# A transposing load cut in two: high and low halves of the attention weights in a hybrid decoder step

## The chip, the cores and the metric

The kernel runs on one core of one Trainium2 chip. The metric is the time of one execution on the device in microseconds (us), measured outside the profiler; for the kernel before it is the median of three runs. A profile is one further execution, which has a time and a span (first to last instruction) of its own.

## What is computed

One layer of a decoder trunk, for a prompt of 2048 tokens and for 64 sample tokens (8 sequences of 8). A projection of the normalised input is split among four mixers (differential attention, a gated recurrence, RWKV-7, a diagonal SSM) and a gate; their outputs are concatenated, gated, projected and added to the input. The change touches the prompt's attention alone:

```python
def diff_attn_core(q, k, v, q_pos, k_pos, lam):
    s = jnp.einsum('bqhcd,bkhcd->bhcqk', q, k).astype(jnp.float32) * (A_QK ** -0.5)
    mask = k_pos[None, :] <= q_pos[:, None]
    p = jax.nn.softmax(jnp.where(mask, s, NEG_BIG), axis=-1)
    w = p[:, :, 0] - lam * p[:, :, 1]
    return jnp.einsum('bhqk,bkhd->bqhd', w.astype(v.dtype), v)
```

There are 4 heads, two score maps (c = 0, 1) of width 32 each, and values of width 64. The kernel keeps float32 accuracy out of 16-bit products: a number is split into a 16-bit high part and a 16-bit rest (low part), and high times high, high times low and low times high are added up.

## The kernel before, in words

The program has four stretches. First (to about 280 us of the profile) the input is normalised and q, k and v are projected. Then, to about 1007 us, `attn_prompt` (L317) works through the prompt's attention while `proj_rest` (L583) projects everything else. After that come the sample's attention with the SSM, and last the RWKV mixer with the output projection. The stage that the change touches is the second.

**Attention.** `attn_prompt` loops over 4 heads, and in each over 16 blocks of 128 queries; a call of `attn_rows` (L350) is one such block, called a row here. Row qb sees (qb + 1) * 128 keys, cut into pieces of at most 512 (`PIECE`): rows 0 to 3 have one piece, rows 4 to 7 two, rows 8 to 11 three, rows 12 to 15 four. That is 16 rows of each length over the four heads, 160 pieces and 544 tiles of 128 keys. For each piece TensorE makes two score maps in PSUM (L363), VectorE takes their maxima (L367), ScalarE their exponentials (L371). When all pieces of a row are there, small VectorE instructions work out a factor for each (L374 to L387). Then, piece by piece: GpSimd scales one map (L391), VectorE scales the other and adds (L392), ScalarE casts the sum to float16, the high part, into the left half of tile `a_w` (L395), GpSimd subtracts it and writes the low part into the right half (L396). One transposing DMA, issued on SP's queue, brings both halves back into `a_wt` with the keys on the partitions (L399), since TensorE needs them so. TensorE then multiplies for each tile of 128 keys the high part with the high and low values (L403, 128 columns) and the low part with the high values (L404, 64 columns), all of a row into one PSUM bank `pv`, of which there is a single buffer (`PVB`). ScalarE and VectorE bring the row's result out (L408, L409). `a_w` and `a_wt` have four buffers each.

**What else SP's queue carries in this stage.** The loads of `kh` (L330) at the start of a head and of `qh` (L335) every four rows, the stores of the projections (L608, L634, L643) and of the packed output weights (L1504). SP works through its instructions in order.

**Filler for TensorE.** `proj_rest` makes 10 groups of columns (`FILL`), 2400 matmuls of mostly 512 columns (L206) in this stage. It is paced: each attention matmul of the loops above is noted in a list, `self.anchors`, as many times as it is worth; the filler's position in its own columns gives an index into that list (function `paced`, L1783, with a lag `LEAD`), and every third filler matmul may only be issued after the attention matmul found there. A piece of n tiles puts 2n entries into the list for its scores and 2n for its products.

**The order on each engine** is not written out by hand: the framework's planner (`schedule_with_timeline_sim=True`, L1956) lays out every engine's instructions when the program is built, by its own estimate of when each can start, under the dependencies and the anchors. At run time each engine then keeps to that order.

Of the kernel before, what the change touches and what calls it, by code (L numbers as in the profile page):

```python
# [23 lines left out]
P = 128  # L24
# [29 lines left out]
class Part:  # L54
# [295 lines left out]
    def attn_rows(self, pool, psum, h, qb, q, kh, dst):  # L350
        nc = self.nc
        nk = (qb + 1) * P
        pieces = [(k0, min(PIECE, nk - k0)) for k0 in range(0, nk, PIECE)]
        np_ = len(pieces)
        mx, l, al = (pool.tile([P, T // PIECE, 2], F32, name=f"a_{k}", bufs=3)[:, :np_] for k in ("mx", "l", "al"))
        es = {}
        sig = self.sig[:, h // 2:h // 2 + 1]
        for p, (k0, kn) in enumerate(pieces):
            ss = []
            for c in range(2):  # L360
                s = psum.tile([P, PIECE], F32, name="s", bufs=SB)
                ss.append(s)
                ins = nc.tensor.matmul(s[:, :kn], q[:, c], kh[:, c, k0:k0 + kn], start=True, stop=True)  # L363
                self.anchors += [ins.ins] * (kn // P)
                if k0 + kn == nk:
                    nc.tensor.matmul(s[:, kn - P:kn], self.identb, self.maskn, start=False, stop=True, skip_group_check=True)
                nc.vector.tensor_reduce(mx[:, p, c:c + 1], s[:, :kn], axis=AX.X, op=ALU.max, negate=True)  # L367
            nc.vector.tensor_scalar(mx[:, p], mx[:, p], sig, None, op0=ALU.mult)  # L368
            for c, s in enumerate(ss):
                e = pool.tile([P, PIECE], F32, name="a_e", bufs=AEB)  # L370
                nc.scalar.activation(e[:, :kn], s[:, :kn], AF.Exp, scale=sig, bias=mx[:, p, c:c + 1],  # L371
                                     accum_out=l[:, p, c:c + 1])
                es[p, c] = e
        if np_ == 1:  # L374
            nc.vector.reciprocal(al[:, 0], l[:, 0])
            nc.vector.tensor_tensor(al[:, 0], al[:, 0], self.lamw, op=ALU.mult)
        else:
            mm = pool.tile([P, 2], F32, name="a_mm", bufs=3)
            bc = mm[:, None, :].to_broadcast([P, np_, 2])
            nc.vector.tensor_reduce(mm, mx.rearrange("p n c -> p c n"), axis=AX.X, op=ALU.min)  # L380
            nc.vector.tensor_tensor(mx, mx, bc, op=ALU.subtract)
            nc.scalar.activation(mx, mx, AF.Exp, scale=-1.0)
            nc.vector.tensor_tensor(l, l, mx, op=ALU.mult)
            nc.vector.tensor_reduce(mm, l.rearrange("p n c -> p c n"), axis=AX.X, op=ALU.add)
            nc.vector.reciprocal(mm, mm)
            nc.vector.tensor_tensor(mm, mm, self.lamw, op=ALU.mult)
            nc.vector.tensor_tensor(al, mx, bc, op=ALU.mult)  # L387
        pv = psum.tile([P, 512], F32, name="pv", bufs=PVB)
        for p, (k0, kn) in enumerate(pieces):
            e0, e1 = es[p, 0], es[p, 1]  # L390
            nc.gpsimd.tensor_scalar(e1[:, :kn], e1[:, :kn], al[:, p, 1:2], 0.0, op0=ALU.mult, op1=ALU.add)  # L391
            nc.vector.scalar_tensor_tensor(e0[:, :kn], e0[:, :kn], al[:, p, 0:1], e1[:, :kn],  # L392
                                           op0=ALU.mult, op1=ALU.add)
            w = pool.tile([P, 2 * PIECE], F16, name="a_w", bufs=AWB)[:, :2 * kn]
            nc.scalar.copy(w[:, :kn], e0[:, :kn])  # L395
            nc.gpsimd.tensor_tensor(w[:, kn:], e0[:, :kn], w[:, :kn], op=ALU.subtract)  # L396
            nt = kn // P
            wt = pool.tile([P, 2 * PIECE // P, P], F16, name="a_wt", bufs=AWT)[:, :2 * nt]
            nc.sync.dma_start_transpose(out=wt, in_=w)  # L399
            for j in range(nt):  # L400
                kt = k0 // P + j
                v = self.vtok[:, kt, h].rearrange("p e d -> p (e d)")
                ins = nc.tensor.matmul(pv[:, :P], wt[:, j], v, start=kt == 0, stop=kt == qb, skip_group_check=True)  # L403
                nc.tensor.matmul(pv[:, :64], wt[:, nt + j], v[:, :64], start=False, stop=kt == qb, skip_group_check=True)  # L404
                self.anchors += [ins.ins] * 2
        un = self.vun[:, h // 2:h // 2 + 1]
        tmp = pool.tile([P, 64], F32, name="a_t", bufs=2)
        nc.scalar.activation(tmp, pv[:, 64:P], AF.Copy, scale=un)  # L408
        nc.vector.scalar_tensor_tensor(dst, pv[:, :64], un, tmp, op0=ALU.mult, op1=ALU.add)  # L409
# [1572 lines left out]
```

## Time and profile before

| | us |
|---|---|
| median of the 3 runs | 1848.69 |
| lowest and highest run | 1846.27, 1848.75 |
| the profiled execution's own time | 1857.33 |
| its span | 1855.5 |
| mean granted TensorE clock | 0.878 of full speed |

| engine | busy us | share of the span |
|---|---|---|
| PE (TensorE matmuls) | 1505.9 | 81% |
| DVE (VectorE) | 1415.4 | 76% |
| ACT (ScalarE) | 902.6 | 49% |
| POOL (GpSimd) | 717.9 | 39% |

The shares are means over stages with different limits; a queue such as SP's is not among them. In the rows below PEld is TensorE's loading of weights, SPq the instructions that SP issues, and text in square brackets is the time the engine stood idle ahead of a row, and what ended it.

### The profile page before, as it was taken

Reading aid. Unit: us, or ns where it says so; the run is one execution under the profiler, and the core shown is the slowest. Engines: PE = TensorE matmul, PEld = TensorE weight load, DVE = VectorE, ACT = ScalarE, POOL = GpSimd, SP = SyncE. Lnnn points to the kernel's source line nnn. Section 1 sums busy time; section 2 is a strip of 40 time slices with the busy share of each in tenths; the row PEclk is TensorE's granted clock in tenths of the full one; section 3 lists DMA queues with packets and bytes.
Section 4 is the critical chain, followed back from the end, with each engine's and each line's share of the span. In section 5 each row is a group of like instructions: output and inputs, shape, how many; then the busy total and the mean of one; then the engine's idle time right before and its main releaser. Section 6 shows DMA issues by size and latency. Waiting matters only on the chain.

```text
span 1855.5 us, 32909 instructions
## 1 busy us (share of the span) xinstructions
PE 1505.9 (81%) x10956; PEld 846.6 (46%) x10956; DVE 1415.4 (76%) x4439; ACT 902.6 (49%) x2211; POOL 717.9 (39%) x807
## 2 busy tenths in 40 slices
PE   5889878788878878888895799856777978888887
PEld 2445644344434434444442355545544544544443
DVE  7797638867888897898786765367787886988975
ACT  3445645555655665666773222243334444444443
POOL 3441312343434553563444444253323433334322
PEclk9999998899989998999897798966687878889889
DMA  4422134655545655473445986655223333233221
GB/s 148 128 87 92 35 109 109 151 117 128 110 117 132 140 150 129 115 162 94 86 105 139 270 268 204 193 170 165 75 66 85 106 90 105 82 91 96 65 85 59
DMA packets 300894, 225.31 MB, mean 121 GB/s; under 512 B 192530, under 2 KB 248564, under 8 KB 300212
## 3 DMA queue, kind: packets, MB, share of 16 engines
q1 hardware_dynamic: 288388, 184.85, 37.5%
q10 hardware_dynamic: 8496, 24.76, 4.6%
q0 software_dynamic: 3840, 13.61, 2.7%
q8 instruction: 86, 1.41, 0.3%
q14 instruction: 84, 0.69, 0.1%
HBM read 130.04 MB, written 53.24 MB: 99 GB/s over the span
## 4 chain that ended last, share of the span: by engine, by line
DVE 29%; PE 18%; DMA 14%; issue 12%; POOL 8%; ACT 4%; SPq 1%; ACTq 0%; POOLq 0%; DVEq 0%
DMA r_zr<-zd 6%; PE acc L206 4%; POOL a_w L396 4%; PE acc L1585 4%; POOL a_e L391 3%; DVE a_mx L367 3%; DMA a_wt<-a_w 2%; DVE a_e L392 2%; DVE r_x16w L1263 2%; DVE r_x L1264 2%; PE ss L512 2%; DMA zd<-r_de 2%; DMA kv<-in_ckv 1%; DVE r_W L1178 1%; ACT a_e L371 1%
## 5 line engine op out<-in xcount | busy, mean ns | idle before, releaser
L206 PE MATMUL acc<-hT,w 128*128 128x512 f16 (+1 forms) x3120 | 636.1, 356 | 39.1 <-DVE shf L628 11.9
L206 PEld LDWEIGHTS <-w 128*128 128x128 f16 x3120 | 271.1, 101 | 341.6 <-issue 70.7
L371 ACT ACTIVATE a_e<-s,a_mx,sig 128x512 f32<-128x512 f32 (+3 forms) x320 | 225.3, 713 | 111.0 <-DVE a_mx L368 88.5
L1585 PE MATMUL acc<-wo,o_h 128*128 128x512 f16 (+1 forms) x816 | 226.6, 424 | 3.5 <-DVE o_h L1563 2.1
L391 POOL TENSOR_SCALAR a_e<-a_e,a_al 128x512 f32<-128x512 f32 (+3 forms) x160 | 115.0, 734 | 287.2 <-DVE a_al L387 232.4
L396 POOL TENSOR_TENSOR a_w<-a_e,a_w 128x512 f16<-128x512 f32 (+3 forms) x160 | 180.2, 1142 | 105.0 <-ACT a_w L395 104.9
L367 DVE TENSOR_REDUCE a_mx<-s 128x1 f32<-128x512 f32 (+3 forms) x320 | 184.2, 601 | 30.7 <-PE s L363 16.5
L392 DVE SCALAR_TENSOR_TENSOR a_e<-a_e,a_al 128x512 f32<-128x512 f32 (+3 forms) x160 | 138.5, 884 | 14.4 <-POOL a_e L391 14.2
L363 PE MATMUL s<-kh,qh 128*128 128x512 f16 (+3 forms) x320 | 101.0, 358 | 40.6 <-ACT a_e L371 36.1
L1585 PEld LDWEIGHTS <-o_h 128*128 128x128 f16 (+1 forms) x816 | 77.5, 106 | 99.4 <-issue 29.3
L403 PE MATMUL pv<-vtok,a_wt 128*128 128x128 f16 x544 | 68.9, 229 | 63.7 <-DMA a_wt<-a_w 52.6
L395 ACT CAST a_w<-a_e 128x512 f16<-128x512 f32 (+3 forms) x160 | 85.7, 558 | 63.6 <-DVE a_e L392 61.9
L1263 DVE TENSOR_TENSOR r_x16w<-r_zr,r_x 128x60 f32<-128x60 f32 (+18 forms) x255 | 59.3, 233 | 54.7 <-DMA r_zr<-zd 51.8
L403 PEld LDWEIGHTS <-a_wt 128*128 128x128 f16 x544 | 51.4, 102 | 88.1 <-DMA a_wt<-a_w 76.3
L1600 POOL TENSOR_TENSOR o_x<-o_y,o_x 128x512 f32<-128x512 f32 (+1 forms) x33 | 48.9, 1496 | 105.6 <-DVE o_y L1598 72.5
L170 POOL TENSOR_TENSOR hT<-hf,hT 128x512 f16<-128x512 f32 (+1 forms) x36 | 36.7, 1026 | 88.5 <-ACT hT L168 86.1
L404 PE MATMUL pv<-vtok,a_wt 128*128 128x64 f16 x544 | 64.9, 200 | 0.0
L371 ACT ACTIVATION_READ_ACCUMULATOR a_e<-s,a_mx,sig 128x1 f32 x320 | 64.2, 201 | 0.0
L1264 DVE TENSOR_TENSOR r_x<-r_x,r_x16w 128x60 f32<-128x60 f32 (+18 forms) x255 | 59.9, 235 | 2.9
L512 PE MATMUL ss<-kv,qbd 128*32 128x256 f32 x256 | 52.7, 415 | 7.9 <-DMA kv<-in_ckv 7.9
L368 DVE TENSOR_SCALAR a_mx<-a_mx,sig 128x2 f32<-128x2 f32 x160 | 58.0, 369 | 0.5
L1365 POOL TENSOR_TENSOR r_sd<-r_Z,r_Dp 64x128 f32<-64x128 f32 x64 | 30.1, 470 | 70.0 <-DVE r_Z L1373 63.5
(545 smaller groups left out, 3201.7 us busy)
## 6 DMA issues: line engine op xcount, KB each, us to landing
kv<-in_ckv SPq DMA_DIRECT2D x128, 256.0 KB
w<-in_w_in ACTq DMA_DIRECT2D x20, 512.0 KB
pc<-pst SPq DMA_DIRECT2D x40, 256.0 KB
xw<-in_xT SPq DMA_DIRECT2D x16, 512.0 KB
w<-in_w_out ACTq DMA_DIRECT2D x16, 512.0 KB
sg<-pst SPq DMA_DIRECT2D x32, 256.0 KB
r_X<-pc SPq DMA_DIRECT2D x16, 512.0 KB
r_zr<-zd SPq DMA_DIRECT2D x16, 512.0 KB
```

Of the source, the lines that this page charges most:

```text
L206: self.nc.tensor.matmul(acc[:, :n], w16[:, k, a, :], h[:, k, e, :], start=(c == 0), stop=(c == 3 * KT - 1))
L363: ins = nc.tensor.matmul(s[:, :kn], q[:, c], kh[:, c, k0:k0 + kn], start=True, stop=True)
L367: nc.vector.tensor_reduce(mx[:, p, c:c + 1], s[:, :kn], axis=AX.X, op=ALU.max, negate=True)
L371: nc.scalar.activation(e[:, :kn], s[:, :kn], AF.Exp, scale=sig, bias=mx[:, p, c:c + 1], accum_out=l[:, p, c:c + 1])
L391: nc.gpsimd.tensor_scalar(e1[:, :kn], e1[:, :kn], al[:, p, 1:2], 0.0, op0=ALU.mult, op1=ALU.add)
L392: nc.vector.scalar_tensor_tensor(e0[:, :kn], e0[:, :kn], al[:, p, 0:1], e1[:, :kn], op0=ALU.mult, op1=ALU.add)
L396: nc.gpsimd.tensor_tensor(w[:, kn:], e0[:, :kn], w[:, :kn], op=ALU.subtract)
L403: ins = nc.tensor.matmul(pv[:, :P], wt[:, j], v, start=kt == 0, stop=kt == qb, skip_group_check=True)
L512: ins = nc.tensor.matmul(sp[g:g + 32, 256 * j:min(256 * j + 256, n)], self.qbd[:, m, s].rearrange("p a q -> p (a q)"), rhs, start=True, st ...
L1263: XV.tensor_tensor(w[:, :, :m], zr[:, k, :, k + 1:], x[:, :, k:k + 1].to_broadcast([P, nu, m]), op=ALU.mult)
L1264: XV.tensor_tensor(x[:, :, k + 1:], x[:, :, k + 1:], w[:, :, :m], op=ALU.add)
L1585: nc.tensor.matmul(a[:n].rearrange("p (c n) -> p c n", c=4), h[:, k, e], self.wo[:, 4 * g:4 * g + 4, k, f, :], start=c == 0, stop=c == 3 * ...
```

## The change

The one transposing load of a piece becomes two, one for the high half and one for the low half. The products are reordered within a piece: all those with high parts come first, then all those with low parts. The anchors are noted one for each product instead of two for each high one, so a piece still notes as many.

```diff
             wt = pool.tile([P, 2 * PIECE // P, P], F16, name="a_wt", bufs=AWT)[:, :2 * nt]
-            nc.sync.dma_start_transpose(out=wt, in_=w)
-            for j in range(nt):
-                kt = k0 // P + j
-                v = self.vtok[:, kt, h].rearrange("p e d -> p (e d)")
-                ins = nc.tensor.matmul(pv[:, :P], wt[:, j], v, start=kt == 0, stop=kt == qb, skip_group_check=True)
-                nc.tensor.matmul(pv[:, :64], wt[:, nt + j], v[:, :64], start=False, stop=kt == qb, skip_group_check=True)
-                self.anchors += [ins.ins] * 2
+            for e in range(2):
+                nc.sync.dma_start_transpose(out=wt[:, e * nt:e * nt + nt], in_=w[:, e * kn:e * kn + kn])
+            for e in range(2):
+                for j in range(nt):
+                    kt, m = k0 // P + j, P >> e
+                    v = self.vtok[:, kt, h].rearrange("p e d -> p (e d)")
+                    ins = nc.tensor.matmul(pv[:, :m], wt[:, e * nt + j], v[:, :m], start=kt == 0 and e == 0,
+                                           stop=kt == qb, skip_group_check=True)
+                    self.anchors.append(ins.ins)
```

## Rows read from the trace of the kernel before

**Rows 1.** Busy time by stage: start and end, length, engines, PEclk, DMA, GB/s.

```profile
280.00:1007.00 727.00, 606.34 (x3994) 307.15 (x3994) 587.80 (x1554) 446.08 (x1094) 322.33 (x336) 0.93 0.53 122
1007.00:1300.00 293.00, 225.43 (x1391) 143.48 (x1388) 187.13 (x542) 85.21 (x226) 125.19 (x139) 0.80 0.69 213
```

**Rows 2.** Waits of the stage: who waited for whom, us in total, times, longest.

```profile
PEld L403 <- DMA a_wt<-a_w: 76.3, 52, 8.6
PE pv L403 <- DMA a_wt<-a_w: 52.6, 38, 8.5
```

**Rows 3.** SP's transposing loads, all 160 of the stage: minimum, median, maximum ns.

```profile
L399 SPq DMA_TRANSPOSE a_wt<-a_w x160: 1167/1239/3051, 286.2 to 1003.5; - x160
```

**Rows 4.** The same line, first row of all (one tile), then a row of four full pieces.

```profile
L399 SPq DMA_TRANSPOSE a_wt<-a_w x1: 1311/1311/1311, 286.2 to 286.2; - x1
...
L399 SPq DMA_TRANSPOSE a_wt<-a_w x4: 1232/1252/1277, 827.1 to 831.4; - x4
```

**Rows 5.** Plain copies on SP's queue in the stage: minimum, median, maximum ns.

```profile
L335 SPq DMA_DIRECT2D qh<-qst x56: 303/425/911, 284.4 to 873.2; - x56
...
L634 SPq DMA_DIRECT2D pc<-pst x50: 319/338/1108, 299.4 to 722.6; - x50
...
L643 SPq DMA_DIRECT2D sg<-pst x40: 319/340/1239, 733.3 to 998.9; - x40
```

**Rows 6.** SP's queue, longest wait in the stage.

```profile
SPq L399 <- POOL a_w L396: 218.3, 82, 9.8
```

**Rows 7.** Head 3, row 7, in order of time: cast, subtraction, loads, first product.

```profile
885.02 1.15 ACT L395 CAST a_w<-a_e 128x512 f16<-128x512 f32 x2
885.73 2.27 POOL L396 TENSOR_TENSOR a_w<-a_e,a_w 128x512 f16<-128x512 f32 x2 [1.79 <-ACT a_w L395]
886.91 2.62 SPq L399 DMA_TRANSPOSE a_wt<-a_w  x2
...
890.63 0.29 PE L403 MATMUL pv<-vtok,a_wt 128*128 128x128 f16 x1 [0.89 <-DMA a_wt<-a_w]
```

**Rows 8.** Two parts of the projected input, first stretch: readers beside writers of hT.

```profile
24.23 2.34 PE L206 MATMUL acc<-hT,w 128*128 128x512 f16 x5
...
26.01 0.62 ACT L168 CAST hT<-hf 128x512 f16<-128x512 f32 x1 [2.90 <-DVE hf L165]
```

**Rows 9.** The last row of the stage (four full pieces), in order of time.

```profile
995.17 0.64 ACT L395 CAST a_w<-a_e 128x512 f16<-128x512 f32 x1
...
997.25 5.36 POOL L396 TENSOR_TENSOR a_w<-a_e,a_w 128x512 f16<-128x512 f32 x4
...
999.36 5.39 SPq L399 DMA_TRANSPOSE a_wt<-a_w  x4
...
1003.48 1.27 SPq L399 DMA_TRANSPOSE a_wt<-a_w  x1
...
1006.57 0.29 PE L403 MATMUL pv<-vtok,a_wt 128*128 128x128 f16 x1 [0.35 <-DMA a_wt<-a_w]
...
1007.13 0.60 POOL L884 DMA_DIRECT2D s5x<-in_st_ssm  x1 [4.52 <-DMA a_wt<-a_w]
```

**Rows 10.** Head 3, row 13: its last load, of two tiles, and the weight load that waited.

```profile
971.18 1.21 SPq L399 DMA_TRANSPOSE a_wt<-a_w  x1
...
973.69 0.10 PEld L403 LDWEIGHTS <-a_wt 128*128 128x128 f16 x1 [0.22 <-DMA a_wt<-a_w]
```

**Rows 11.** Head 3, row 12: TensorE at its first and its second piece.

```profile
955.41 0.23 PE L403 MATMUL pv<-vtok,a_wt 128*128 128x128 f16 x1 [1.25 <-DMA a_wt<-a_w]
...
955.76 2.11 PE L206 MATMUL acc<-hT,w 128*128 128x512 f16 x9
957.71 0.22 PE L403 MATMUL pv<-vtok,a_wt 128*128 128x128 f16 x1
```

**Rows 12.** A stretch in which TensorE mostly waited, and the one behind it (columns as in 1).

```profile
530.00:538.00 8.00, 2.77 (x30) 1.22 (x28) 7.97 (x18) 6.97 (x17) 5.11 (x6) 0.74 0.10 20
538.00:545.00 7.00, 6.85 (x19) 2.52 (x20) 6.76 (x25) 2.68 (x8) 4.72 (x6) 0.56 0.58 146
```

## The prediction

> **What bounds the kernel now.** I read the busy time by stage first. The change acts in the second stage, 280 to 1007 us, and there TensorE is busy 606 of 727 us, VectorE 588, ScalarE 446, GpSimd 322 [rows 1]: two engines near their limit, and some 120 us in which TensorE has nothing. The waits of the stage say where part of that goes: 38 times a product with the attention weights stood idle for its transposing load, 52.6 us together, 1.38 us each; on the weight-load side it is 52 times and 76.3 us [rows 2]. With 160 pieces, a third of them reach TensorE no sooner than it needs them, and a later landing is felt there at once. The other two thirds have some slack, as the second piece of [rows 11], whose products came after nine filler matmuls.
>
> Next I read SP's queue, whose instructions count in no engine's busy share. A transposing load holds it 1.24 us in the median [rows 3], and its size does not matter: 1.31 us for the first row, with one tile of 128 keys, and 1.25 us in the median for four full pieces [rows 4]. A plain copy holds it 0.34 to 0.43 us [rows 5]. The 160 loads take 198 us of the stage, and the 146 copies shown some 54, so SP is issuing about a third of the time. Its longest wait is for GpSimd's low parts, 82 times, 218 us [rows 6]: SP itself is mostly early.
>
> **What it removes.** A high half need no longer wait for the low one. In [rows 7] the cast of the high part released GpSimd at 885.73 us and the load was issued at 886.91; the high load could have gone 1.18 us sooner. This rests on the planner telling the halves of one tile apart. The trace shows that it does for another tile: TensorE reads hT at 24.23 us while ScalarE writes a later part of it at 26.01 [rows 8]. Half a load also lands sooner. A load of a full piece (eight 128x128 blocks) issued at 1003.48 us let its products start at 1006.57, after 3.09 us [rows 9]; one of four blocks, as a full half will be, took from 971.18 to 973.69, 2.51 us [rows 10]. So a first high half lands 1.18 + 0.58 = 1.76 us sooner than its piece does now.
>
> **What it adds.** 160 more transposing loads, at 160 x 1.24 = 198 us of SP's time. They pass the other copies of that queue, whose delay I cost at nothing as long as two qh and three store buffers cover a few microseconds; where a head begins, its single kh is loaded behind the last row's loads, at most four more of them, and 3 starts x 4 x 1.37 = 16 us bound that; I take 0, because kh is free as soon as the old head's last scores are done, ahead of those loads. Back to back, loads start 1.37 us apart: (1003.48 - 999.36) / 3 [rows 9]. Within a row the pieces already leave at that pace, so the row has no room for twice as many. A row of n full pieces now lands its last load (n - 1) x 1.37 + 3.09 us after the first is issued. Afterwards the first is issued 1.18 us sooner, there are 2n, and the last low half lands after (2n - 1) x 1.37 - 1.18 + 2.51. The difference is n x 1.37 - 1.76: 0.39 us sooner with one piece, later by 0.98 with two, 2.35 with three and 3.72 with four. With 16 rows of each length the late ones add up to 16 x (0.98 + 2.35 + 3.72) = 113 us.
>
> **How much of that reaches the end.** The bounds are 0 (filler hides all) and 113. I take a third, 38 us, since a third of the pieces stand just in time today [rows 2]; two thirds have slack and filler between pieces. Of the 16 two-piece rows I then take nothing, as 0.98 us is less than the nine filler matmuls of [rows 11] last, 2.11 us: 5 off, 33 left.
>
> Against it stands the earlier arrival. Where a first piece makes TensorE wait, its four high products, within 0.35 us [rows 11], now run sooner, but the low ones behind them land only 0.39 us sooner, and the row's PSUM bank stays open until they are through. I give half of the 52 waits to first pieces, which are 64 of the 160: 26 x 0.39 = 10 us saved; the bounds are 0 and 26 us, half of the 52.6.
>
> The end of the stage is exposed: nothing is left there to fill with, and the next stage's loads wait for the last products [rows 9]. The casts of that row begin at 995.17 us. If SP starts on the first high half by 996, its eighth load starts at 1005.6 and lands at 1008.1, 1.5 us after now; if it starts behind the stores, at 999.36 as now, the eighth starts at 1008.95 and lands at 1011.5, 4.9 later. I take 3.
>
> The products cost nothing: the same 1088, of the same shapes, only in another order, and the anchors keep their number. But half a piece's anchors are now low products, so the filler hung on these comes later: a second wait for every piece, with less behind it that may go ahead.
>
> The sum is 33 - 10 + 3 = +26 us. The profiled execution took 1857.33 us (span 1855.5) and would take 1883; it lies 8.6 above the median of the runs, so for the median I say 1848.7 + 26 = **1875 us**.
>
> TensorE's clock can add to a wait: where TensorE worked 2.77 of 8 us, it was granted 0.74 of full speed, and in the 7 us behind that 0.56, near the lower of its two levels, while it was busy 6.85 us [rows 12]. I put no price of its own on that, as the third is rough enough to hold it.
>
> The Trainium skill, page "DMA: Bandwidth & Descriptors", section "Issuing engines are not separate DMA queues", says that the sequencer's time to start a DMA is usually small beside the DMA itself. Here the trace disagrees: 1.24 us of the 3.09 from issue to use. By that rule the added loads would delay nothing, and the first rival would be the forecast, some 50 us lower than mine.
>
> **The rivals.** *The low halves hide (faster).* High halves land 1.76 us sooner, more than the mean wait of 1.38; the planner puts scores and filler between the high and the low products of a piece, and no low half is ever late. Then half of the 52.6 us goes and the end costs 1.5: 1848.7 - 26 + 1.5 = 1824 us. For it: SP is issuing only a third of the time, and the two-piece rows have the cover. Against: three- and four-piece rows leave back to back already, and what is anchored to low products cannot stand ahead of them. It decides if low halves land less than about 1 us after TensorE comes to them.
>
> *No change.* Losses in the long rows and gains in the short ones cancel, within 0.2% (3.7 us, about what a measurement of this kernel can tell from no change): 1849 us.
>
> *SP becomes the bound of the long rows (slower, dearer).* Eight loads at 1.37 us are 11 us a row, and with stores and qh behind them nothing has slack: all 113 us and 4.9 at the end, 1967 us. Against: the 32 rows of three and four pieces share much of 727 us, so a row has more than 11.
>
> *The high half does not go sooner* (the change doesn't do what it says): if the planner makes its load wait for the whole tile, the 1.18 us is lost and every row is late by n x 1.37 - 0.58, 182 us over 64 rows; a third of that and 4.9 make 1914 us. [rows 8] speak against.
>
> **How the numbers follow.** The forecast gets 0.49, the dearer case 0.07, the unsplit tile 0.08: 0.64 for slower by over 0.2%. The faster rival gets 0.23, since what reaches TensorE depends on how the planner lays the filler anew, which no row shows; no change gets 0.13. The range must reach into both sides: from 1831, most of the way to the faster case, to 1922, past the unsplit tile. Left out are about half of the faster case and the dearest. The forecast's own range, with a tenth to six tenths of the 113 us felt, is 1853 to 1910.
>
> **What would show it.** Right: 320 transposing loads at 1.2 us on SP's queue whatever their size; high loads released by ScalarE; the gap from the last cast of a long row to its last product longer by 2 to 4 us; waits for a_wt above 52.6 us in total, now at L403's low products; the stage longer by about 26 us with the stages behind it the same. Wrong: loads of half the size that hold SP for half the time, or low products that never wait. If the stage gets shorter, what failed is the third that I let through to TensorE.

## The result and the profile after

The changed kernel takes 1864.69 us (median of 4 runs, 1858.98 to 1866.26) beside 1848.72 for the kernel before in the same measurement: a ratio of 1.0076, 95% interval 1.0051 to 1.0101 (14 us by the ratio, 16 by the medians). It is slower, inside the forecast range and ten microseconds below the forecast of 1875. Timed once more on another occasion, the ratio was 1.0143 (1.0106 to 1.018). The two intervals do not overlap, so the price is best told as 0.8 to 1.4%, or 14 to 26 us.

The profile of the changed kernel is of its fastest run, 1858.98 us (span 1857.2, clock 0.879), while that of the kernel before was 8.6 us above its median; the two differ by 1.7 us only. So the accounts below use a second profile of each as well, called "again", taken together (1842.14 and 1866.77 us, spans 1840.3 and 1865.0).

Busy time by stage in the changed kernel, to be read beside [rows 1]:

```profile
280.00:1007.00 727.00, 612.94 (x3941) 307.17 (x3941) 586.18 (x1541) 442.54 (x1088) 325.84 (x339) 0.91 0.51 121
1007.00:1300.00 293.00, 227.50 (x1492) 147.03 (x1490) 184.55 (x548) 85.81 (x226) 125.63 (x136) 0.84 0.69 215
```

In the attention stage TensorE got through fewer instructions (3941 for 3994) in more busy time, and its clock is 0.91 for 0.93: it worked more slowly, it did not wait more. The waits say the same. Those for the transposed weights, to be read beside [rows 2]:

```profile
PEld L405 <- DMA a_wt<-a_w: 81.0, 78, 5.1
PE pv L405 <- DMA a_wt<-a_w: 48.5, 50, 4.8
```

They are more often but shorter, and the two rows together make 129.5 us where they made 76.3 + 52.6 = 128.9. All loads of SP's queue (minimum, median, maximum ns), beside [rows 3]:

```profile
L400 SPq DMA_TRANSPOSE a_wt<-a_w x320: 1119/1206/2705, 283.2 to 1001.4; - x160
```

Twice as many, each half the size, 1.21 us each. And the end of the stage in order of time, beside [rows 9] (the L405 products of the last row are left out):

```profile
991.35 0.62 ACT L395 CAST a_w<-a_e 128x512 f16<-128x512 f32 x1 [0.37 <-DVE a_e L392]
992.00 11.62 SPq L400 DMA_TRANSPOSE a_wt<-a_w  x8
...
992.95 5.83 POOL L396 TENSOR_TENSOR a_w<-a_e,a_w 128x512 f16<-128x512 f32 x4
...
1003.71 13.26 SPq L645 DMA_DIRECT2D sg<-pst  x7
...
1005.53 0.60 POOL L886 DMA_DIRECT2D s5x<-in_st_ssm  x1 [6.76 <-DMA a_wt<-a_w]
...
1005.64 8.66 PE L206 MATMUL acc<-hT,w 128*128 128x512 f16 x48
...
1014.61 0.57 PE L206 MATMUL acc<-hT,w 128*128 128x64 f16 x14
```

The first high half is loaded 0.03 us after its cast ends (991.97), before GpSimd has begun the low half; eight loads follow back to back. What is new is at the bottom: when the last row's weights are there (1005.53), 62 filler matmuls are still to come, and seven stores stand behind the eight loads. In the kernel before the filler was through at 994, ahead of the last products; now it ends at 1015, alone. The next stage feels it through SP's queue: in the kernel before its first loads, of kv, are issued at 1007.42, 0.03 us after the last product ends; now at 1017.23, behind the seven stores, the last of which holds a result of that filler.

**Where the time went.** The pair of profiles "again", each with the first score product of the sample's attention, and the first and the eleventh load of r_zr in the output stretch. The kernel before:

```profile
1006.78 1.06 PE L512 MATMUL ss<-kv,qbd 128*32 128x256 f32 x2
...
1223.27 0.76 SPq L1222 DMA_DIRECT2D r_zr<-zd  x1
...
1314.27 0.60 SPq L1222 DMA_DIRECT2D r_zr<-zd  x1
```

The changed kernel:

```profile
1022.94 1.03 PE L514 MATMUL ss<-kv,qbd 128*32 128x256 f32 x2 [6.16 <-DMA kv<-in_ckv]
...
1238.83 0.76 SPq L1224 DMA_DIRECT2D r_zr<-zd  x1
...
1337.89 0.60 SPq L1224 DMA_DIRECT2D r_zr<-zd  x1
```

It is 16.2 us late when the sample's attention begins, still 15.6 late at the first r_zr, 23.6 late at the eleventh, and 24.7 late at the end of the span. So there are two losses: 16 us in the attention stage and 8 us in the 100 us at the start of the output stretch. The first pair agrees on the two places but not on the sizes, 8.3 and 6.7 us; between them its kernel before took 11.8 us longer, so that at the end of the span only 1.7 are left. One profile carries that much chance: in the five profiles of kernels with one load a piece, that first score product ends between 1002.0 and 1014.4 us. In the three of kernels that cut every load, with three store buffers on SP's queue, it ends at 1022.7, 1023.5 and 1029.0, beyond that band.

The stage's 16 us, by busy time from 280 us to the last attention or filler matmul, first the kernel before (again):

```profile
280.00:1000.40 720.40, 603.73 (x3996) 306.14 (x3995) 587.86 (x1544) 444.25 (x1093) 322.03 (x337) 0.93 0.53 123
```

and the changed one (again):

```profile
280.00:1016.80 736.80, 617.32 (x4000) 309.28 (x3999) 591.63 (x1562) 445.74 (x1094) 326.16 (x340) 0.91 0.52 121
```

The stage is 16.4 us longer; TensorE is busy 13.6 us more for the same work, and idle only 2.8 us more (119.5 for 116.7). The first pair of profiles gives the same: from 280 us to the last matmul it was busy 606.7 us before and 621.1 after, and idle 120.7 and 114.1. By this account the loss of the stage is the same work at a lower clock, not waiting.

For the second loss, VectorE's share of the stretch from the first to the eleventh load of r_zr, the kernel before (again) and then the changed one (again):

```profile
1223.30:1314.30 91.00, 66.78 (x551) 52.41 (x549) 72.19 (x242) 35.14 (x98) 36.11 (x49) 0.62 0.41 118
...
1238.80:1337.90 99.10, 66.95 (x554) 52.56 (x553) 75.86 (x254) 38.60 (x107) 36.47 (x50) 0.64 0.41 113
```

The planner puts more of VectorE's instructions ahead of the eleventh load (254 for 242, busy 3.7 us more), and VectorE stands idle 4.4 us more. The same holds over all profiles: in the seven of them in which the two loads are 98 to 104 us apart, VectorE runs 253 to 260 instructions between them, and in the seven in which they are 90 to 92 apart, 242 in each.

### The profile page after: what moved, and what is told of

It is laid out like the page before. It is cut to its first block, busy times and chain, and to the rows that moved or that the text cites. A ratio compares the mean times of both kernels' runs of the same rounds, so it can differ in the third digit from the quotient of the medians.

```text
span 1857.2 us, 33215 instructions
## 1 busy us (share of the span) xinstructions
PE 1507.4 (81%) x10956; PEld 843.5 (45%) x10956; DVE 1404.5 (76%) x4439; ACT 902.8 (49%) x2211; POOL 715.9 (39%) x807
## 4 chain that ended last, share of the span: by engine, by line
DVE 28%; PE 18%; DMA 16%; issue 11%; POOL 6%; ACT 5%; SPq 2%; ACTq 0%; POOLq 0%; DVEq 0%
DMA r_zr<-zd 5%; PE acc L206 4%; PE acc L1587 4%; DVE a_mx L367 4%; DMA a_wt<-a_w 3%; POOL a_w L396 3%; DVE a_e L392 3%; DVE r_x16w L1265 2%; ACT a_e L371 2%; DMA kv<-in_ckv 2%; POOL a_e L391 2%; DVE r_x L1266 2%; DMA zd<-r_de 2%; DVE r_W L1180 1%; PE ss L514 1%
## 5 line engine op out<-in xcount | busy, mean ns | idle before, releaser
L391 POOL TENSOR_SCALAR a_e<-a_e,a_al 128x512 f32<-128x512 f32 (+3 forms) x160 | 119.9, 764 | 288.5 <-DVE a_al L387 221.6
L405 PE MATMUL pv<-vtok,a_wt 128*128 128x64 f16 (+1 forms) x1088 | 88.9, 217 | 66.5 <-DMA a_wt<-a_w 48.5
L363 PE MATMUL s<-kh,qh 128*128 128x512 f16 (+3 forms) x320 | 110.2, 381 | 32.0 <-ACT a_e L371 27.8
L405 PEld LDWEIGHTS <-a_wt 128*128 128x128 f16 x1088 | 67.9, 103 | 117.9 <-DMA a_wt<-a_w 81.0
L368 DVE TENSOR_SCALAR a_mx<-a_mx,sig 128x2 f32<-128x2 f32 x160 | 59.4, 380 | 0.5
L514 PE MATMUL ss<-kv,qbd 128*32 128x256 f32 x256 | 46.5, 404 | 13.5 <-DMA kv<-in_ckv 13.5
L44 PE MATMUL ra<-r_W,r_F 64*128 64x128 f32 x256 | 35.8, 332 | 26.1 <-DVE r_F L1183 26.1
```

The source lines that it names most:

```text
L405: ins = nc.tensor.matmul(pv[:, :m], wt[:, e * nt + j], v[:, :m], start=kt == 0 and e == 0, stop=kt == qb, skip_group_check=True)
```

## The experiments

Four theories stand in the expectations. A is the forecast's: twice as many loads make the low halves late, and TensorE waits for them. B: the new order of products and anchors costs. C: the planner lays out everything anew, behind the stage too. D was formed after the first four runs: the added loads push the projection's stores back on SP's queue, the three store buffers (pst) fill, the filler stops, TensorE's clock falls, and the filler that is left runs alone at the end. Ratios are to the kernel before in the same measurement, with 95% intervals.

**Both kernels again.** No edit.

> The kernel before, unchanged, for a second profile and the scatter of one: every theory expects 1.000 within 0.2%. Its attention stage (last product with the weights, last filler matmul) should end within 2 us of the first profile's 1007 and 994 us; if it does not, single profiles tell nothing of a dozen microseconds.

> The changed kernel, unchanged, for a second profile: 1.005 to 1.010. Theory A (SP's queue makes low halves late and the stage longer): the stage ends later than in the kernel before by 10 to 15 us. Theory C (the planner, given other estimates, lays everything behind the change anew, and the time is made anywhere): the stage is no longer than before, and the time is lost behind it.

Measured: 0.9988 (0.9964 to 1.0012) and 1.0143 (1.0106 to 1.018). The kernel before ended its attention stage 7 us earlier than in its first profile (1000.4 for 1007.4, the filler at 987.1 for 994.2), not within the 2 us expected. So one pair of profiles tells nothing of a dozen microseconds, and the sizes above stand only where several profiles agree. The changed kernel is slower than the 1.005 to 1.010 expected, and its stage ends later, as A says and C does not.

**One half of the change at a time.** The order alone, with the old load:

```diff
-            for e in range(2):
-                nc.sync.dma_start_transpose(out=wt[:, e * nt:e * nt + nt], in_=w[:, e * kn:e * kn + kn])
+            nc.sync.dma_start_transpose(out=wt, in_=w)
```

> One load for a piece, as before; only the products go in the new order (all high ones, then all low ones), with an anchor for each. Theory A (the added loads cost, SP's queue): 1.000, within 0.2%. Theory B (filler hung on low products comes too late, whatever the loads): 1.004 to 1.010, as the whole change. Theory C (planner's luck): anything within 0.5% either way, and the stretches behind 1010 us differ as much as the stage.

Measured: 0.9986 (0.9965 to 1.0008). And the two loads alone, with the old order of products:

```diff
-            for e in range(2):
-                for j in range(nt):
...
-                    self.anchors.append(ins.ins)
+            for j in range(nt):
...
+                self.anchors += [ins.ins] * 2
```

> Two loads for a piece, but the products in the old order, high and low by turns, so that the first low product comes after one high one. Theory A: 1.005 to 1.012, at least as slow as the whole change, since TensorE has less to do between a first high and a first low product. Theory B: 1.000 to 1.003. Theory C: within 0.5% either way.

Measured: 1.0134 (1.01 to 1.0169), the whole of the change, though a little more than A's range. B falls: the order costs nothing and gains nothing; the loads cost everything.

**What SP's queue does.** With that, SP's queue of the two "again" kernels in order of time, over the start of the fourth head; before:

```profile
804.46 6.36 SPq L399 DMA_TRANSPOSE a_wt<-a_w  x4
810.91 2.15 SPq L330 DMA_DIRECT2D kh<-kst  x4
813.11 1.83 SPq L335 DMA_DIRECT2D qh<-qst  x4
815.63 1.83 SPq L643 DMA_DIRECT2D sg<-pst  x2
821.42 5.56 SPq L399 DMA_TRANSPOSE a_wt<-a_w  x4
827.07 1.01 SPq L643 DMA_DIRECT2D sg<-pst  x2
```

and after:

```profile
817.46 10.76 SPq L400 DMA_TRANSPOSE a_wt<-a_w  x8
828.31 1.94 SPq L330 DMA_DIRECT2D kh<-kst  x4
830.29 1.84 SPq L335 DMA_DIRECT2D qh<-qst  x4
834.09 13.07 SPq L400 DMA_TRANSPOSE a_wt<-a_w  x8
847.25 0.53 SPq L335 DMA_DIRECT2D qh<-qst  x1
848.16 10.32 SPq L400 DMA_TRANSPOSE a_wt<-a_w  x8
858.54 1.51 SPq L335 DMA_DIRECT2D qh<-qst  x3
860.30 5.05 SPq L400 DMA_TRANSPOSE a_wt<-a_w  x4
865.45 1.93 SPq L335 DMA_DIRECT2D qh<-qst  x4
867.82 5.08 SPq L400 DMA_TRANSPOSE a_wt<-a_w  x4
872.99 1.50 SPq L645 DMA_DIRECT2D sg<-pst  x3
```

Before, two stores follow each group of loads. After, five groups of loads (32 of them) pass before a store of the projections is issued; the last one had been issued at 813.7, 59.3 us earlier (the longest such gap before is 17.3 us). Since then three results have been completed (VectorE's part of them begins at 818.6, 825.63 and 833.33), so the three store buffers are full. ScalarE begins a fourth at 831.66 and a fifth at 840.34, and writes into a store buffer again only behind the stores (order of time on ScalarE, all but these two left out):

```profile
840.34 0.68 ACT L642 ACTIVATE pth<-acc,wsc 128x512 f32<-128x512 f32 x1
...
876.66 0.90 ACT L643 ACTIVATE pst<-acc,wsc 128x64 f32<-128x64 f32 x2
```

These two are 36 us apart, and no filler matmul stands in TensorE's order between 837.0 and 877.2. TensorE waits at none of them: the planner put none there, which fits that its estimate had the buffers full too. What that does to TensorE's clock, from busy time in the first profile of the changed kernel, where the same gap lies at 834 to 874 us:

```profile
834.00:846.00 12.00, 6.54 (x54) 4.08 (x52) 10.71 (x33) 5.75 (x18) 5.64 (x7) 0.85 0.65 130
846.00:877.00 31.00, 19.95 (x86) 8.64 (x87) 29.62 (x107) 25.21 (x74) 14.52 (x19) 0.51 0.44 96
877.00:884.00 7.00, 6.98 (x47) 3.60 (x46) 6.07 (x14) 4.36 (x11) 5.26 (x6) 1.00 0.49 115
```

After 12 us in which it was busy for 6.54, TensorE was granted half its clock (1.2 GHz) for nearly 31 us, and the full clock once the filler was back. A second gap, 18.8 us from 466.5, comes with 20.5 us at half clock, from 470.2. Before, no gap in the filler is longer than 8.6 us.

**Tests of D: the stores off SP's queue.** The edit, in the changed kernel and, as a control, in the one before:

```diff
-        st_q = nc.sync
+        st_q = nc.scalar
```

> The changed kernel, with the stores of the projections (L610, L636, L645) issued on ScalarE's queue instead of SP's. Theory A (low halves land late and TensorE waits for them): SP carries 100 copies of 0.34 us less, 34 of some 490 us, so most of the loss stays, 1.008 to 1.014. Theory D (the added loads starve the stores on SP's queue; with three store buffers the filler stops, up to 40 us at a head's start, TensorE's clock falls, and the filler left over runs alone at the end of the stage): no filler gap above some 10 us, the last filler matmul before the last product of the attention, and 0.995 to 1.003.

Measured: 1.0212 (1.0163 to 1.0261), above the range of either theory.

> The kernel before with the same move of the stores, as the control: ScalarE gets 100 issues of about 0.35 us, SP is relieved of them. Both theories: 0.995 to 1.005, since SP issues only a third of the stage here. What after_stores_act loses against this one is the price of the cut load alone: A says 10 us or more, D within 5.

Measured: 1.0037 (1.0011 to 1.0063). In the changed kernel the gaps are gone as D says (the longest is 9.8 us), but the attention itself is slower: its last product comes at 1036.7 us, against 1006.5 in the control. Of these 30 us TensorE is busy 18.3 more (621.0 for 602.7, at a clock of 0.91 for 0.94) and idle 11.9 more, so its clock fell with no long gap in the filler. ScalarE, which now issues the stores, waits 90.0 us for the maxima (a_mx, L368) where it waits 63.6 in the control, and TensorE's waits for the weights are 87.5 + 60.0 us, against 86.9 + 54.6 in the control. Why stores on ScalarE's queue cost little in the kernel before and 30 us in this one was not found; 6 us more of waits for weights do not make A's case, and the run speaks against D as the only way in which the added loads cost.

**Tests of D: more store buffers.** Again in both kernels:

```diff
-                    st = pool.tile([P, 512], F32, name="pst", bufs=3)
+                    st = pool.tile([P, 512], F32, name="pst", bufs=6)
```

> The changed kernel with six store buffers (pst) instead of three, stores still on SP. Theory A: as the changed kernel, 1.010 to 1.018. Theory D: the filler can go three more blocks, some 15 us, before it stops, so gaps of 40 and 19 us shrink to about 25 and 4 us and a third to a half of the loss goes: 1.004 to 1.010.

Measured: 1.0051 (1.0017 to 1.0084).

> The kernel before with six store buffers (pst) instead of three: the control of after_pst6 (1.0051). Theory D (the cut loads' loss is mostly filler that stops for want of a store buffer): the kernel before never lacks one for long (its longest filler gap is 8.6 us), so 0.998 to 1.002, and the cut's price with six buffers is the 0.3 to 0.7% left. Theory A (the price is the late low halves whatever the buffers): six buffers help this kernel as much as they helped the changed one, 0.988 to 0.993.

Measured: 1.0007 (0.9981 to 1.0034). Six buffers are worth nothing to the kernel before, as D says and A does not; the changed one loses 0.5% with them where it lost 0.8 and 1.4%. Its interval lies below that of the second measurement and overlaps that of the first. No gap in the filler over 8 us is left, where D expected one of 25, though the stores still come up to 42.9 us apart. Over the start of the fourth head ScalarE keeps taking filler results out (order of time on ScalarE):

```profile
829.94 0.68 ACT L643 ACTIVATE pst<-acc,wsc 128x512 f32<-128x512 f32 x1
...
837.00 0.68 ACT L643 ACTIVATE pst<-acc,wsc 128x512 f32<-128x512 f32 x1
...
844.30 0.69 ACT L643 ACTIVATE pst<-acc,wsc 128x512 f32<-128x512 f32 x1
...
854.80 0.68 ACT L643 ACTIVATE pst<-acc,wsc 128x512 f32<-128x512 f32 x1
```

and TensorE keeps its clock (busy time by stretch: the whole stage, then the stretch that was at half clock):

```profile
280.00:1004.80 724.80, 606.48 (x3996) 305.25 (x3995) 590.82 (x1555) 447.63 (x1094) 325.91 (x336) 0.94 0.52 123
...
847.00:875.00 28.00, 24.88 (x139) 11.53 (x139) 24.23 (x85) 20.68 (x57) 10.53 (x12) 0.94 0.36 91
```

The stage is as long as that of the kernel before, with all 320 loads in it. So this run and its control bear D out for the stage: not late weights but late stores; the run with the stores on ScalarE's queue is the one against it. What stays shows behind the stage: the first and the eleventh r_zr are 103.7 us apart, where they are 90.2 to 92.3 in the five profiles of kernels with one load a piece.

**The loads for which nothing waits.** One load for a whole piece as before, and beside it one of the high half into a tile that is never read, so that this kernel does more than is needed:

```diff
             nc.sync.dma_start_transpose(out=wt, in_=w)
+            wx = pool.tile([P, 2 * PIECE // P, P], F16, name="a_wx", bufs=2)[:, :nt]
+            nc.sync.dma_start_transpose(out=wx, in_=w[:, :kn])
```

> The kernel before with one more transposing load behind each, of the high half into a tile that nobody reads: the same 320 loads on SP's queue, but no product waits for the added ones and the products keep their order. It does more than the kernel needs. Theory A: the main load of a later piece still goes later, by up to (n - 1) x 1.37 us in a row of n pieces, half of the change's effect on products: 1.003 to 1.008. Theory D: the queue is as full as with the change, so the store gaps at the starts of heads 2 and 4, the filler gaps and the loss are those of the change: 1.009 to 1.016.

Measured: 1.0193 (1.0129 to 1.0256), above both ranges. 320 loads cost here too, but this run is less clean than meant: the unread load needs the high half alone, so the planner puts it ahead of the one that is read (at the first piece 285.3 against 286.7 us), which is late by that. The waits for a_wt are 100.4 + 64.4 us, 39 more than in the kernel before again (75.0 + 51.1). The stage, to 1029.3 us, is 28.9 us longer than there, and 25.3 of that is idle time of TensorE (142.0 us); it is busy only 3.5 more. Gaps in the filler of 14.3 and 28.2 us show D's stop of the filler, but the loss is mostly waiting, 13.3 us of it ahead of products with the weights, and such waits do not grow in the changed kernel.

**Short and long rows.** The load cut only in rows of one and two pieces, then only in rows of three and four (`np_ > 2` in place of `np_ <= 2`):

```diff
-            for e in range(2):
+            for e in range(2) if np_ <= 2 else ():
                 nc.sync.dma_start_transpose(out=wt[:, e * nt:e * nt + nt], in_=w[:, e * kn:e * kn + kn])
+            if not (np_ <= 2):
+                nc.sync.dma_start_transpose(out=wt, in_=w)
```

> The changed kernel with the load cut only in rows of one or two pieces (48 loads more instead of 160); rows of three and four pieces have one load for a piece; three store buffers, products in the new order everywhere. Theory A: one-piece rows land 0.4 us sooner, two-piece rows 1.0 us later, both covered: 0.997 to 1.002. Theory D: it is the short rows at the start of a head that fill SP's queue without a break, so the filler gap at a head's start stays above 10 us in part: 1.003 to 1.009.

Measured: 1.007 (1.0042 to 1.0098).

> The changed kernel with the load cut only in rows of three and four pieces (112 loads more). Theory A: all the late landings are here, 1.9 to 2.4 us a row: 1.009 to 1.016, as the whole change. Theory D: the queue has room at the head's start again, so no filler gap above 10 us, and 1.002 to 1.008.

Measured: 1.007 (1.0044 to 1.0096). By A's arithmetic only the long rows should cost. Both cost the same, which A cannot give. Both times lie in D's ranges, but not for D's reason: it laid the gap to the short rows, and it is the long rows that show one, 21.1 us at 827 us, with the stage's end at 1012.9 us. The short rows have no gap over 10.7 us, and that one is at 396 us and not at the start of a head; they end the stage at 1005.5, as the kernel before does. What is seen of their loss is behind it (98.3 us from the first to the eleventh r_zr, 97.9 for the long rows).

**A version that might beat both.** Only the first piece's load cut, and six store buffers:

```diff
-            for e in range(2):
+            for e in range(2) if p == 0 else ():
                 nc.sync.dma_start_transpose(out=wt[:, e * nt:e * nt + nt], in_=w[:, e * kn:e * kn + kn])
+            if not (p == 0):
+                nc.sync.dma_start_transpose(out=wt, in_=w)
...
-                    st = pool.tile([P, 512], F32, name="pst", bufs=3)
+                    st = pool.tile([P, 512], F32, name="pst", bufs=6)
```

> Cuts the load of a row's first piece alone (64 added loads instead of 160, products with high parts first as in the change) and gives the projection stores six pst buffers. It is tried as a version that may beat both. By the prediction's arithmetic a row's first high half lands 1.76 us sooner, and its last load n x 1.37 less (n - 1) x 1.37 less 1.18 us, that is 0.19 us, later (0.39 sooner with one piece). Theory A (late low halves make TensorE wait): nothing is late any more, so 26 x 0.39 us or about 10 us are saved: 0.993 to 1.000 of the kernel before. Theory D (the added loads starve the projection stores): the buffers cover it, no filler gap over 12 us, 0.995 to 1.001. Theory C (whatever changes the attention's loads makes the planner lay out the output stretch anew): the first to the eleventh r_zr load in that stretch lie 97 to 104 us apart instead of 91, and the time is 1.002 to 1.006 although the stage ends no later than before.

Measured: 1.0046 (1.0023 to 1.0069). No gap in the filler over 8 us, as D says, but no gain either: the time lies outside D's range and A's, and A's saving does not come. C's time is met and its sign is not, as the eleventh r_zr is 91.7 us behind the first. Where this kernel loses its 0.5% was not found. No version that ran was faster than the kernel before.

## Why the prediction was right, and where it was not

The sign, the range and, within ten microseconds, the size were right; the main term of the sum was not.

- **The loads: right.** 320 at 1.21 us in the median, of half the size. The rule of the Trainium skill that the prediction weighed (page "DMA: Bandwidth & Descriptors", section "Issuing engines are not separate DMA queues": the time to start a DMA is usually small beside the DMA) disagrees with the runs here, where a load of either size holds the queue 1.2 us, and the forecast that followed it, 50 us lower, did not come.
- **The high half goes sooner: right.** In the last row its load follows the cast by 0.03 us, and over the stage SP's longest wait is now for ScalarE's casts (46 times, 100.9 us; for GpSimd's low parts 49 times, 37.7 us, where it was 218.3 [rows 6]). So the rival of the unsplit tile is out.
- **When the last load of a row lands: right in its direction, at half to four fifths of the size; the single piece gains nothing.** From the end of the row's first cast to that landing, mean of 16 rows each, in the profiles again:

| pieces | before us | after us | forecast of the difference | measured |
|---|---|---|---|---|
| 1 | 4.73 | 4.69 | -0.39 | -0.04 |
| 2 | 6.63 | 7.11 | 0.98 | 0.48 |
| 3 | 8.94 | 10.80 | 2.35 | 1.86 |
| 4 | 10.85 | 12.84 | 3.72 | 1.99 |

- **"I take a third", 33 us net of 5: this term failed.** The 52.6 us for which products stood idle for their load, and the 48.5 in the changed kernel, divide into those at first and those at later pieces of a row (first pair of profiles). At later pieces they are 18.5 us before and 25.7 after, a loss of 7.2 where 33 was forecast. The low halves are late, as worked out, and 27.0 of the 48.5 us are now waits for them, but the planner had laid other work ahead of most of their products. So the sign "waits above 52.6 us in total" did not come. The rival that the low halves hide was right in this and wrong in what it concluded.
- **The earlier arrival, 10 us: right for the wait that it names.** At first pieces these waits fell from 34.1 to 22.8 us, a saving of 11.3. But the same products then waited for other things: all idle time ahead of them, whatever ended it, fell from 44.9 to 40.2 us only.
- **The gap from the last cast of a long row to its last product: near the sign.** It grew by 1.4 us with three pieces and 2.3 with four (again), 2 to 4 forecast.
- **The step that hid the larger part of the cost** is the sentence that the delay of SP's other copies counts "at nothing as long as two qh and three store buffers cover a few microseconds". The condition was stated and not worked out: at a head's start the last row of four pieces and the first short rows stand close together, and with twice the loads the stores come 59 us apart, not a few. That fills three buffers; with six the stage has its old length.
- **"I put no price of its own" on TensorE's clock:** this was the larger part of the stage's loss. Of 16.4 us, 13.6 are the same work at a lower clock; idle time grew by 2.8 (in the first pair 14.4, and idle time fell by 6.6).
- **The end of the stage: right in its size, wrong in what ends it.** From the first cast of the last row to the release of the next stage's load it is 1005.53 - 991.35 = 14.18 us, and was 1007.13 - 995.17 = 11.96 [rows 9]: 2.2 more, 3 forecast. But the stage then waits for filler, not for that row.
- **"The stages behind it the same": wrong.** About 8 us of 24.7 came there. Over the stretch that loses them, the order that the planner gives VectorE is the same in the kernel before, with the new product order alone and with six buffers, and another in each kernel that cuts loads. Another order alone does not cost: in the kernel before with its stores on ScalarE's queue, with the unread loads and with only first pieces cut it is another too, and the stretch is 90.7, 90.9 and 91.7 us long. The long stretches are those in which VectorE has more instructions to run in it, 3.7 us of work in the pair above; why its idle time grows by 4.4 beside that, and why the planner orders it so, is not settled.

So the forecast of +26 us came near the measured 14 to 26 by luck. Its own three terms, as measured, make 7.2 - 11.3 + 2.2 = -1.9 us. Half the reason was its own, a queue on which twice the loads take twice the time; but that was felt through the stores, TensorE's clock and a new layout behind the stage, none of which the sum has.

## What to carry to other kernels

When a DMA is cut in two, count the time on the issuing queue first, then list everything else that this queue carries and ask of each how many buffers stand between it and the engine that fills them. A stall in work that only fills gaps is not free: here TensorE's clock fell to half in the gap, and what was not done there was done alone later. Where a planner lays out the program, time a part of the change alone and look behind the stage as well.

## What the runs showed of the hardware

- A transposing load holds SP's queue for 1.12 us at the least and 1.21 in the median with half the bytes, 1.24 with all of them [rows 3]: cutting it in two doubles what the queue spends on it.
- TensorE stayed at half its clock for nearly 31 us while it was busy 19.95 of 31 us, and was back at the full clock in the 7 us in which it was busy for 6.98. In this stage the changed kernel lost more through the clock (13.6 us of busy time for the same work) than through idle time (2.8 us).
- The same kernel, profiled twice, ended its attention stage 7 us apart (1007.4 and 1000.4 us), and the first pair of profiles differs by hardly more at the stage's end (1007.4 and 1015.2): alone it shows little beyond the scatter.
